# Down projections of a decoder layer: seven half-size products over 16 of 22 weight blocks, with the weight sums made by adding DMAs

## The chip, the cores and the metric

The kernel runs on one core of a Trainium2 chip. The core has a matrix engine (TensorE, "PE" in the profile; "PEld" is its weight load), a vector engine (VectorE, "DVE"), a scalar engine (ScalarE, "ACT"), a general engine (GpSimd, "POOL") and a sequencer that issues DMAs (SyncE, "SP"). Matmuls read SBUF and write PSUM, which has eight banks of 128 x 512 float32. The metric is the device time of one execution in microseconds; smaller is better.

## What is computed

The reference is one layer of a decoder trunk on a sequence of 512 tokens with model width 1024 (float32): a half-step SwiGLU network, a mixer (dilated attention beside an mLSTM, gated and projected), and a second half-step SwiGLU network. The part that matters here is SwiGLU, which stands twice:

```python
def swiglu(x, w_gate, w_up, w_down):
    return (jax.nn.silu(x @ w_gate) * (x @ w_up)) @ w_down

f = swiglu(rmsnorm(x, ffn1_pre_g[l]), ffn1_w_gate[l], ffn1_w_up[l], ffn1_w_down[l])
x = x + 0.5 * rmsnorm(f, ffn1_post_g[l])
```

The inner width is 2816, which is 22 blocks of 128. The down projection is a product of (512 tokens x 2816) with (2816 x 1024).

## The kernel before

**Precision.** Each float32 operand is split in a high part (ScalarE casts it to the matmul's 32-bit type) and a residue (VectorE subtracts the high part). A product is then three matmuls: high x high, residue x high, high x residue. Buffers of high parts are called `wh`, `xh`, `ah`, residues `wl`, `xl`, `al`; each kind has five buffers in turn, and the float32 weight blocks as they land (`wf`, printed `B_a`, `wf_ad`) have three.

**The down stage.** Its output, 512 x 1024, fills all eight banks: four tiles of 128 tokens by two halves of the columns. The names are by quarter of the output: `acca` (tokens 0 to 255, left columns), `accc` (the same tokens, right columns), `accb` (tokens 256 to 511, left), `accd` (those, right). The 22 blocks of the inner width are worked in three ways:

- Blocks 0 to 11 by seven half-size products instead of eight (Strassen's method in Winograd's form). Tokens, inner width and columns are halved. The inner halves are cut in three groups of two blocks each (`HALF = 6`), so there are 7 x 3 products. The string `STEPS` names them: "52" is product 5 of group 2. Product 1 multiplies first-half activations with block (0,0), product 2 second-half activations with block (1,0), product 3 with block (1,1); products 5, 6, 7 and 4 take sums of activation quarters and sums of weight blocks. `sums` makes these sums on VectorE: the weight sums in a tile T (in the place of `hTh`, the transposed input of gate and up, which is used up by then), the activation sums in a tile S.
- Blocks 12 to 14 (`FILL`) as half steps "p" (tokens 0 to 255) and "q" (tokens 256 to 511), strewn among the products.
- Blocks 15 to 21 as plain chunks in `down`: 15 to 17 at once, and the last four (`KEEP`) held back, so that each token tile is finished as a whole and its norm can start.

Every step, a product or a half fill, is twelve matmuls of 128 x 512; a plain chunk is 24.

**What sets the order.** `Down.run` writes the order out by hand: for each step in `STEPS` the load of a later step's block, the sums and casts of the step two ahead, the residues of the next one, the product, and `middle`, which copies or adds finished products among the banks. `Order` (printed as L250, its call) keeps that order on each engine, and each engine works strictly in its order. The first steps are put into the end of the gate/up stage (`seven`, L325, drives them by `next(ahead)`). Loads go on SP's queue. After the stage `down` (L230 is its matmul) does the plain chunks and `PostNorm` (L162, L167), whose gain rows are loaded on GpSimd's queue by `begin`.

Of the kernel before, what the change touches and what calls it, by code (L numbers as in the profile page):

```python
# [39 lines left out]
def tile_hybrid_block(ctx: ExitStack, tc: tile.TileContext, a: dict):  # L40
# [111 lines left out]
    class PostNorm:  # L152
        def __init__(self, t, g, where, name, half=False):
            self.t, self.g, self.name, self.half = t, g, f"p{name}{t}", half
# [3 lines left out]
        def bank(self, acc, b):  # L158
# [3 lines left out]
            nc.vector.tensor_tensor(self.fg[:, BANKS[b]], acc[b], self.g[:, BANKS[b]], op=ALU.mult)  # L162
# [37 lines left out]
    def down(n, chunk_src, get_x, post, finish, todo, name, accs=None, first=0, late=lambda: None):  # L200
        pins = []
        held = []
        accs = accs or [pair(f"acc_{name}{t}") for t in range(NT)]
        for kk in range(first, n):
            xh, xl = get_x(kk)
            wh, wl = load_w(chunk_src(kk), f"{name}d{kk}")
            if kk < n - KEEP:
                for t in range(NT):
                    for b in range(2):
                        step(accs[t][b], xh, xl, wh, wl, t, b, kk == 0, False)  # L210
                    if kk == first and t == 1:
                        late()
# [71 lines left out]
    def seven(do, fs, wgu, x, low, scr, aT, name, ahead):  # L284
# [76 lines left out]
        for i in range(len(fs)):  # L361
# [37 lines left out]
            if w:  # L399
# [11 lines left out]
    LOADS = {"1": ((0, 0),), "2": ((1, 0),), "5": ((0, 1),), "6": ((1, 1),), "7": ((0, 0),), "3": ((1, 1),),  # L411
             "4": ((1, 0),)}
# [4 lines left out]
    class Down:  # L417
        after = FILL[-1] + 1

        def __init__(self, do, wdq, wd, aT, scr, name):  # L420
            self.do, self.wdq, self.wd, self.aT, self.scr, self.name = do, wdq, wd, aT, scr, name
            self.xp, self.src, self.x, self.w, self.wf = None, {}, {}, {}, {}
            self.accs = [[None, None] for _ in range(NT)]
            self.n = 0

        def tt(self, out, p, q, op):
            self.do("vector", "tensor_tensor", out, p, q, op=op)

# [8 lines left out]
        def room(self, n):  # L437
            self.n += 1
            if self.xp and self.n % 2:
                return self.xp.tile([P, 2, T], F32, tag="bf", bufs=3, name=n)  # L440
            return act.tile([P, 2, T], F32, tag="wf", bufs=3, name=n)

        def fetch(self, s):
            if s[0] in "pq":
                t = self.room(f"B{s}_{self.name}").rearrange("p a b -> p (a b)")
                self.do("sync", "dma_start", t, self.wd[FILL[int(s[1])]])
                self.src[s] = self.aT[:, FILL[int(s[1])], None, slice(0, H) if s[0] == "p" else slice(H, T)], halves(t, T)
            for k, j in LOADS.get(s[0], ()):
                t = self.room(f"B{k}{j}_{self.name}{s}")
                self.do("sync", "dma_start", t, halves(self.wdq[int(s[1]), k, j], T))  # L450
                self.wf[s[1], k, j] = t

        def sums(self, s, early=False):
            k, g = s[0], int(s[1])
            if k in "pq":
                return
            A, B = (lambda i, j: self.A(i, j, g)), (lambda i, j: self.wf[s[1], i, j])
            x = A(*{"1": (0, 0), "2": (0, 1), "4": (1, 1)}.get(k, (0, 0)))
            w = B(*{"1": (0, 0), "2": (1, 0), "3": (1, 1)}[k]) if k in "123" else None
            if k in "64":  # L460
                w = self.T[:, 2 * g:2 * g + 2, :]
            if early:
                w = self.scr.tile([P, 2, Q], F32, tag="cd", bufs=1, name=f"t1_{self.name}")
                x = self.scr.tile([P, 2, Q], F32, tag="ab", bufs=1, name=f"s1_{self.name}")[:, :, :H]
            elif k in "57":
                x, w = halves(self.S[:, 7, :], H), self.T[:, 6:8, :]
            if k == "5":
                self.t1, self.s1 = w, x
                self.tt(w, B(0, 1), B(0, 0), SUB)
                self.tt(x, A(1, 0), A(1, 1), ADD)  # L470
            elif k == "6":
                x = halves(self.S[:, g, :], H)
                self.tt(w, B(1, 1), self.t1, SUB)
                self.tt(x, self.s1, A(0, 0), SUB)
            elif k == "7":
                self.tt(w, self.T[:, 2 * g:2 * g + 2, :], B(0, 0), SUB)
                self.tt(x, A(0, 0), A(1, 0), SUB)
            elif k == "3":
                x = work.tile([P, 2, H], F32, tag="s4", bufs=1, name=f"s4_{self.name}{g}")
                self.tt(x, A(0, 1), halves(self.S[:, g, :], H), SUB)  # L480
            elif k == "4":
                self.tt(w, B(1, 0), w, SUB)
            self.src[s] = x, w

        def cast(self, s, which):
# [4 lines left out]
            self.do("scalar", "copy", halves(hl[0], v.shape[2]), v)  # L490
            (self.w if which == "w" else self.x)[s] = hl

        def low(self, s, which):
            v = self.src[s][which == "w"]
            h, l = (halves(y, v.shape[2]) for y in (self.w if which == "w" else self.x)[s])
            self.tt(l, v, h.bitcast(F32), SUB)
# [20 lines left out]
        def middle(self, s):  # L517
            q1, p5 = self.S[:, 3:5, :], self.S[:, 5:7, :]
            for i in range(2):
                if s == "12":  # L520
# [67 lines left out]
    def ffn(pool, todo, first_w, hT, wgu, wdq, wd, post, finish, name, begin=None, pins=(), aT=None):  # L588
# [43 lines left out]
        if begin:  # L632
            begin()
# [883 lines left out]
```

## Time and profile before

| | |
|---|---|
| median of 3 runs | 1346.76 us (1346.64 to 1346.85) |
| the profiled execution | 1346.88 us, its span 1345.1 us, granted TensorE clock 0.999 |
| TensorE busy | 1334.8 us (99%) |
| VectorE busy | 1009.6 us (75%) |
| ScalarE busy | 630.5 us (47%) |
| GpSimd busy | 37.2 us (3%) |

A row of the profile names a line of the kernel, an engine, an operation and tiles as output<-inputs. Tile names end in `_a` in the first FFN and `_b` in the second. A start is in us from the start of the span; "[0.38 <-ACT xh_a L250]" behind a row is idle time of its engine before it and what ended it. Matmuls are pipelined, so that the duration of one (0.39 us for 512 columns) is longer than the distance to the next.

### The profile page before, as it was taken

Reading aid. Unit: us, or ns where it says so; the run is one execution under the profiler, and the core shown is the slowest. Engines: PE = TensorE matmul, PEld = TensorE weight load, DVE = VectorE, ACT = ScalarE, POOL = GpSimd, SP = SyncE. Lnnn points to the kernel's source line nnn. Section 1 sums busy time; section 2 is a strip of 40 time slices with the busy share of each in tenths; the row PEclk is TensorE's granted clock in tenths of the full one; section 3 lists DMA queues with packets and bytes.
Section 4 is the critical chain, followed back from the end, with each engine's and each line's share of the span. In section 5 each row is a group of like instructions: output and inputs, shape, how many; then the busy total and the mean of one; then the engine's idle time right before and its main releaser. Section 6 shows DMA issues by size and latency. Waiting matters only on the chain.

```text
span 1345.1 us, 20741 instructions
## 1 busy us (share of the span) xinstructions
PE 1334.8 (99%) x8319; PEld 1202.5 (89%) x8319; DVE 1009.6 (75%) x1531; ACT 630.5 (47%) x1018; POOL 37.2 (3%) x64
## 2 busy tenths in 40 slices
PE   9999999999999999999999999999999999999998
PEld 8999999878998888888888889999889999998786
DVE  7999897996755557475756676776379998997983
ACT  6444444554643544544544444344265444444552
POOL 1000000000300000000000000000010000000000
PEclk9999999999999999999999999999999999999999
DMA  5333333654433422412222212335312333235441
GB/s 197 99 98 110 110 96 110 234 182 147 128 104 115 142 78 94 156 64 79 79 78 78 79 47 79 103 101 196 134 57 87 109 110 110 95 110 202 173 141 63
DMA packets 42720, 153.96 MB, mean 114 GB/s; under 512 B 4836, under 2 KB 4844, under 8 KB 42368
## 3 DMA queue, kind: packets, MB, share of 16 engines
q1 hardware_dynamic: 39456, 140.56, 31.7%
q0 software_dynamic: 3152, 12.08, 2.7%
q8 instruction: 65, 1.06, 0.3%
q14 instruction: 31, 0.25, 0.1%
q10 hardware_dynamic: 16, 0.00, 0.0%
HBM read 146.33 MB, written 6.29 MB: 113 GB/s over the span
## 4 chain that ended last, share of the span: by engine, by line
PE 90%; DVE 6%; issue 2%; ACT 1%; DMA 0%; DVEq 0%; POOLq 0%; ACTq 0%; SPq 0%
PE qb_b L325 10%; PE qb_a L325 10%; PE pq L175 8%; PE pm L175 7%; PE p L175 6%; PE qa_b L325 4%; PE qa_a L325 4%; PE qb_gm L1075 4%; PE acc_o L230 3%; PE pvo L1201 2%; PE pvo L1203 2%; PE pvo L1202 2%; PE pg_a L189 2%; PE pq L189 2%; PE pg_b L189 2%
## 5 line engine op out<-in xcount | busy, mean ns | idle before, releaser
L175 PE MATMUL pq<-hTh_mx,wh_qk 128*128 128x512 f32 x160 | 63.2, 395 | 0.0
L175 PE MATMUL pq<-hTl_mx,wh_qk 128*128 128x512 f32 x160 | 62.4, 390 | 0.0
L92 DVE TENSOR_TENSOR wl_qk<-wf_qk,wh_qk 128x1024 fp32r<-128x1024 f32 x24 | 29.4, 1223 | 33.3 <-ACT wh_qk L90 16.7
L175 PE MATMUL pm<-hTh_mx,wh_mqk 128*128 128x512 f32 x128 | 50.3, 393 | 0.0
L1201 PE MATMUL pvo<-wh_vo,hTh_mx 128*128 128x512 f32 x128 | 50.2, 392 | 0.0
L175 PE MATMUL pm<-hTl_mx,wh_mqk 128*128 128x512 f32 x128 | 49.9, 390 | 0.0
L1203 PE MATMUL pvo<-wl_vo,hTh_mx 128*128 128x512 f32 x128 | 49.9, 390 | 0.0
L1202 PE MATMUL pvo<-wh_vo,hTl_mx 128*128 128x512 f32 x128 | 49.8, 389 | 0.0
L92 DVE TENSOR_TENSOR wl_mqk<-wf_mqk,wh_mqk 128x1024 fp32r<-128x1024 f32 x16 | 19.6, 1224 | 35.4 <-ACT wh_mqk L90 26.4
L90 ACT CAST wh_qk<-wf_qk 128x1024 fp32r<-128x1024 f32 x24 | 25.0, 1047 | 43.0 <-issue 11.6
L175 PE MATMUL pq<-hTh_mx,wl_qk 128*128 128x512 f32 x160 | 39.6, 389 | 0.0
L250 ACT CAST wh_a<-cd_a 128x1024 fp32r<-128x1024 f32 x19 | 20.0, 1050 | 40.9 <-DVE cd_a L250 40.9
L250 ACT CAST wh_b<-cd_b 128x1024 fp32r<-128x1024 f32 x19 | 20.0, 1050 | 40.5 <-DVE cd_b L250 40.5
L325 PE MATMUL qa_a<-hTh_f,wh_a 128*128 128x256 f32 x152 | 38.2, 284 | 0.0
L325 PE MATMUL qa_b<-hTh_f,wh_b 128*128 128x256 f32 x152 | 38.2, 284 | 0.0
L325 PE MATMUL qa_b<-hTl_f,wh_b 128*128 128x256 f32 x152 | 38.1, 283 | 0.0
L325 PE MATMUL qa_a<-hTl_f,wh_a 128*128 128x256 f32 x152 | 38.1, 283 | 0.0
L996 DVE SCALAR_TENSOR_TENSOR z<-pm,cw,z 128x511 f32<-128x511 f32 (+2 forms) x48 | 35.3, 744 | 1.4 <-ACT z L994 0.9
L90 ACT CAST wh_mqk<-wf_mqk 128x1024 fp32r<-128x1024 f32 x16 | 16.8, 1051 | 41.2 <-PE pvo L1202 22.6
L175 PEld LDWEIGHTS pq<-hTh_mx,wl_qk 128*128 128x128 f32 x160 | 30.0, 188 | 6.2
L175 PEld LDWEIGHTS pq<-hTh_mx,wh_qk 128*128 128x128 f32 x160 | 30.1, 188 | 6.0
L175 PEld LDWEIGHTS pq<-hTl_mx,wh_qk 128*128 128x128 f32 x160 | 30.1, 188 | 6.0
(746 smaller groups left out, 4555.8 us busy)
## 6 DMA issues: line engine op xcount, KB each, us to landing
wf_qk<-in_wqk SPq DMA_DIRECT2D x24, 512.0 KB, 3.3
B_a<-in_wdq SPq DMA_DIRECT2D x21, 512.0 KB, 3.4
B_b<-in_wdq SPq DMA_DIRECT2D x21, 512.0 KB, 3.4
g_a<-in_wgu SPq DMA_DIRECT2D x19, 512.0 KB, 3.8
u_a<-in_wgu SPq DMA_DIRECT2D x19, 512.0 KB, 3.8
g_b<-in_wgu SPq DMA_DIRECT2D x19, 512.0 KB, 3.8
u_b<-in_wgu SPq DMA_DIRECT2D x19, 512.0 KB, 3.7
wf_mqk<-in_wmqk SPq DMA_DIRECT2D x16, 512.0 KB, 3.4
```

The lines of the kernel that those rows point to most:

```text
L90: nc.scalar.copy(wh, wf)
L92: nc.vector.tensor_tensor(wl, wf, wh.bitcast(F32), op=ALU.subtract)
L175: nc.tensor.matmul(out, lhsT=wt[:, k * P:(k + 1) * P], rhs=x[:, k, 0:T], start=n == 0, stop=n == len(terms) - 1)
L189: nc.tensor.matmul(outs[b][:, tok], lhsT=ws_[b][w][:, k * P:(k + 1) * P], rhs=x[:, k, tok], start=i + k + hf == 0, stop=hf == 1 and i == 2 ...
L230: nc.tensor.matmul(out, lhsT=x[:, tk], rhs=w[:, cs], start=first and n == 0, stop=last and n == 2, skip_group_check=True)
L250: self.last[eng] = getattr(getattr(nc, eng), fn)(*args, **kw).ins
L325: nc.tensor.matmul(out, lhsT=wt[:, i * P:(i + 1) * P], rhs=y[:, i, :], start=first and n == 0, stop=last and n == len(terms) - 1, skip_gro ...
L996: nc.vector.scalar_tensor_tensor(z[:, s:], src[:, :T - s], cw[:, ct, 3 - s:4 - s], z[:, s:], op0=ALU.mult, op1=ALU.add)
L1075: nc.tensor.matmul(out, lhsT=wt[:, i * P:(i + 1) * P], rhs=y[:, i, :], start=first and m == 0, stop=last and m == len(terms) - 1, skip_gro ...
L1201: nc.tensor.matmul(out, lhsT=hTh[:, k, tk], rhs=wh[:, cs], start=k == 0, stop=False)
L1202: nc.tensor.matmul(out, lhsT=hTl[:, k, tk], rhs=wh[:, cs], start=False, stop=False)
L1203: nc.tensor.matmul(out, lhsT=hTh[:, k, tk], rhs=wl[:, cs], start=False, stop=k == KD - 1)
```

## The change

Sixteen blocks instead of twelve go through the seven products (`HALF = 8`, four groups: 28 products), two blocks (16 and 17) are half steps, and the last four are plain chunks, all of them held. The signs of the activation sums are turned, and the right half of the output columns is computed with the opposite sign, so that every weight sum is a sum without a minus: 00 + 01 for product 5, that + 11 for product 6, that + 10 for product 4, and 11 + 01 for product 7 ((k,j) is inner half k, column half j). The chain is then made by DMAs that add: block (0,0) is loaded straight into T for product 1; when its residue is made, GpSimd issues a DMA that adds block (0,1) to it in place, and so on. Product 7's chain stands on product 3's block, loaded into four tiles `u3` in the places of scratch tiles. VectorE makes no weight sum any more. Its order is by `front` (sums and casts, three steps ahead) and `back` (residues, two ahead). The fill and plain blocks get their right halves negated in the cast (`flip`), and `PostNorm` multiplies the right bank by -1. `middle` has new places, and `late` is gone. The gains are loaded behind the `u3` loads. `Order`'s line is L263 now, and `step`'s L243.

```diff
-    def load_w(src, name, n=1024, after=()):
+    def cast_w(wh, wf, flip=False):
+        if not flip:
+            return nc.scalar.copy(wh, wf)
+        nc.scalar.copy(wh[:, :T], wf[:, :T])
+        return nc.scalar.mul(wh[:, T:], wf[:, T:], -1.0)
+
+    def load_w(src, name, n=1024, after=(), flip=False):
...
-            nc.scalar.copy(wh, wf)
+            cast_w(wh, wf, flip)
...
-            nc.vector.tensor_tensor(wl, wf, wh.bitcast(F32), op=ALU.subtract)
+            m = T if flip else n
+            nc.vector.tensor_tensor(wl[:, :m], wf[:, :m], wh[:, :m].bitcast(F32), op=ALU.subtract)
+            if flip:
+                nc.vector.scalar_tensor_tensor(wl[:, T:], wf[:, T:], -1.0, wh[:, T:].bitcast(F32), op0=ALU.mult,
+                                               op1=ALU.subtract)
...
-    HALF = 6
-    FILL = (12, 13, 14)
-    STEPS = "20 21 10 50 60 11 51 61 12 52 62 22 p0 p1 70 30 p2 71 31 72 32 40 41 42 q0 q1 q2".split()
...
+    HALF = 8
+    FILL = (16, 17)
+    STEPS = ("20 21 10 11 12 13 22 50 51 52 53 23 60 61 62 63 p0 30 31 32 33 70 71 72 73 p1 "
+             "40 41 42 43 q0 q1").split()
+    BLOCK = {"1": (0, 0), "2": (1, 0), "3": (1, 1), "5": (0, 1), "6": (1, 1), "7": (0, 1), "4": (1, 0)}
...
+        def add(self, s):
+            g = int(s[1])
+            out = halves(self.u3[g], T) if s[0] == "7" else self.U(g)
+            self.do("gpsimd", "dma_start", out, self.B(g, BLOCK[s[0]]), accum_op=ADD)
+
+        def behind(self, s):
+            g = s[1]
+            if s[0] in "153":
+                self.add({"1": "5", "5": "6", "3": "7"}[s[0]] + g)
+            if s == "13":
+                self.fetch("23", "gpsimd")
+            if s == "53":
+                self.fetch("p0", "gpsimd")
+                for g in range(4):
+                    t = self.u3[g] = work.tile([P, D], F32, tag=TEMPS[g], bufs=1, name=f"u3_{self.name}{g}")
+                    self.do("gpsimd", "dma_start", halves(t, T), self.B(g, BLOCK["3"]))
+                if self.begin:
+                    with tc.issue_after(self.do.last["gpsimd"]):
+                        self.begin()
+                self.fetch("p1")
+            if s == "33":
+                for g in range(4):
+                    self.add(f"4{g}")
+                self.fetch("q0")
+                self.fetch("q1")
...
             if k == "5":
-                self.t1, self.s1 = w, x
-                self.tt(w, B(0, 1), B(0, 0), SUB)
-                self.tt(x, A(1, 0), A(1, 1), ADD)
+                self.tt(x, A(1, 1), A(1, 0), SUB)
             elif k == "6":
-                x = halves(self.S[:, g, :], H)
-                self.tt(w, B(1, 1), self.t1, SUB)
-                self.tt(x, self.s1, A(0, 0), SUB)
+                self.stt(x, x, A(0, 0), SUB)
+            elif k == "3":
+                self.stt(x, A(0, 1), x, SUB)
             elif k == "7":
-                self.tt(w, self.T[:, 2 * g:2 * g + 2, :], B(0, 0), SUB)
+                x = work.tile([P, 2, H], F32, tag="s3", bufs=2, name=f"s3_{self.name}{g}")
                 self.tt(x, A(0, 0), A(1, 0), SUB)
...
         def middle(self, s):
...
+            q1, p5 = self.S[:, 4:6, :], self.S[:, 6:8, :]
+            k = {"13": "1", "53": "5", "63": "5", "73": "1", "42": "2", "q1": "6"}.get(s)
+            for i in range(2 if k else 0):
+                out = self.out[k][i]
+                if s in ("13", "53"):
+                    self.do("scalar", "copy", (q1 if s == "13" else p5)[:, i, :], out)
+                elif s in ("63", "73"):
+                    self.tt(out, self.out["6"][i], p5[:, i, :], ADD)
+                else:
+                    self.tt(out, out, q1[:, i, :], ADD)
+            if s == "53":
+                self.tt(p5, p5, q1, ADD)
...
+            for g in range(4):
+                self.do("sync", "dma_start", self.U(g), self.B(g, BLOCK["1"]))
             yield
+            self.added = self.lowered = 2
+            self.front(2)
+            self.back(2)
             self.product(s1)
             yield
+            for n in range(2, len(STEPS)):
+                lead = 2 if n < 5 else 3
+                self.front(n + lead)
+                self.back(n + lead - 1)
                 self.product(STEPS[n])
                 self.middle(STEPS[n])
...
-            return PostNorm(t, gains[0], tbuf[t % 2], "f1", True)
+            return PostNorm(t, gains[0], tbuf[t % 2], "f1", True, True)
```

The instructions move in three places. GpSimd's queue in the first down stage, before: after the opening's last square root (`r_f`) only the two gain rows are loaded, and the next is a constant of the mixer.

```order
L104 TENSOR_TENSOR r_f_223<-s_3_213,nhalf 128x1
L97 DMA g_f1post<-in_ffn_post_g 128x1024
L97 DMA g_mpre<-in_mix_pre_g 128x1024
L1151 DMA selr<-in_sel 4x512
L104 TENSOR_TENSOR r_pf_3755<-v_pf_3753,nhalf 128x1
```

The same place now; the rows onto T are adding DMAs (for products 5, 6 and 4), and so are the second four onto `u` (product 7; the first four are plain loads for product 3).

```order
L263 DMA T_a<-in_wdq 128x1024 x4
L263 DMA B_a<-in_wdq 128x1024
L263 DMA T_a<-in_wdq 128x1024 x4
L263 DMA Bp_a<-in_wd 128x1024
L263 DMA u_a_3158<-in_wdq 128x1024
...
L263 DMA u_a_3164<-in_wdq 128x1024
L107 DMA g_f1post<-in_ffn_post_g 128x1024
L107 DMA g_mpre<-in_mix_pre_g 128x1024
L263 DMA u_a_3158<-in_wdq 128x1024
...
L263 DMA u_a_3164<-in_wdq 128x1024
L263 DMA T_a<-in_wdq 128x1024 x4
```

Twenty-four DMAs stand where two stood, sixteen of them adding ones, and the gains come after the second four adds. VectorE's order before, where group 2's weight sums are made (`T_a<-B_a`) and products 5 and 6 of it prepared (S are activation sums, `wl` and `xl` residues):

```order
L250 TENSOR_TENSOR T_a<-B_a_3063,B_a_3041 128x1024
L250 TENSOR_TENSOR S_a<-aT_a 128x512
L250 TENSOR_TENSOR wl_a<-B_a_3041,wh_a 128x1024
L250 TENSOR_TENSOR xl_a<-aT_a,xh_a 128x512
L250 TENSOR_TENSOR T_a<-B_a_3087,T_a 128x1024
L250 TENSOR_TENSOR S_a<-S_a,aT_a 128x512
L250 TENSOR_TENSOR wl_a<-T_a,wh_a 128x1024
L250 TENSOR_TENSOR xl_a<-S_a,xh_a 128x512
L250 TENSOR_TENSOR wl_a<-T_a,wh_a 128x1024
L250 TENSOR_TENSOR xl_a<-S_a,xh_a 128x512
```

VectorE's order now, from the sum of the two saved products (behind the copy of product 5, step 53) to the banks that step p0 adds into:

```order
L263 TENSOR_TENSOR S_a<-S_a 128x1024
L263 SCALAR_TENSOR_TENSOR S_a<-S_a,aT_a 128x512
L263 TENSOR_TENSOR wl_a<-T_a,wh_a 128x1024
L263 TENSOR_TENSOR xl_a<-S_a,xh_a 128x512
L263 SCALAR_TENSOR_TENSOR S_a<-S_a,aT_a 128x512
...
L263 TENSOR_TENSOR wlp_a<-Bp_a,whp_a 128x512
L263 SCALAR_TENSOR_TENSOR wlp_a<-Bp_a,whp_a 128x512
L263 TENSOR_TENSOR xlp_a<-aT_a,xhp_a 128x256
L263 SCALAR_TENSOR_TENSOR S_a<-aT_a,S_a 128x512
L263 TENSOR_TENSOR wl_a<-u_a_3158,wh_a 128x1024
L263 TENSOR_TENSOR xl_a<-S_a,xh_a 128x512
L263 TENSOR_TENSOR accc_a_2935<-accb_a_2937,S_a 128x512
```

No row makes a weight sum any more; the whole queue behind the saved sum now starts when step 53 is done, and the bank sum of step 63 stands behind the residues of 30.

More of the change, by code (lines that the diff above doesn't have):

```diff
@@ L198, in new_hT, with down @@
         return hTh, hTl
[L200 removed]
+    def down(n, chunk_src, get_x, post, finish, todo, name, accs=None, first=0):
         pins = []
         held = []
+        flip = accs is not None
         accs = accs or [pair(f"acc_{name}{t}") for t in range(NT)]
@@ L489, in cast @@
             hl = [pool.tile([P, n], F32R, tag=f"{tag}{y}", bufs=5, name=f"{which}{y}{s}_{self.name}")[:, :n_] for y in "hl"]
-            self.do("scalar", "copy", halves(hl[0], v.shape[2]), v)
+            h = halves(hl[0], v.shape[2])
+            if which == "w" and s[0] in "pq":
+                self.do("scalar", "copy", h[:, 0, :], v[:, 0, :])
+                self.do("scalar", "mul", h[:, 1, :], v[:, 1, :], -1.0)
+            else:
+                self.do("scalar", "copy", h, v)
             (self.w if which == "w" else self.x)[s] = hl
```

151 lines of the change are left out of this document (57 added, 94 removed).

## The prediction

> **What bounds the kernel now.** I read the page's engine table and chain of waits first, then TensorE's instructions in order of time through the two down stages, then who waited for whom there.
>
> ```profile
> span 1345.1 us, 20741 instructions
> PE 1334.8 (99%) x8319; PEld 1202.5 (89%) x8319; DVE 1009.6 (75%) x1531; ACT 630.5 (47%) x1018; POOL 37.2 (3%) x64
> PE 90%; DVE 6%; issue 2%; ACT 1%; DMA 0%; DVEq 0%; POOLq 0%; ACTq 0%; SPq 0%
> ```
>
> TensorE sets the end: it carries 90% of the chain. So two things alone can change the time: how many matmuls there are, and where TensorE waits. Both stand in the timeline of the down stages (start, duration, matmuls merged in a row):
>
> ```profile
> 236.97 1.09 PE L514 MATMUL acca_a<-wh_a,xh_a 128*128 128x512 f32 x4
> ...
> 241.15 1.09 PE L514 MATMUL acca_a<-wh_a,xh_a 128*128 128x512 f32 x4
> ...
> 243.90 1.07 PE L514 MATMUL accd_a<-wh_a,xh_a 128*128 128x512 f32 x4
> ...
> 246.62 1.07 PE L514 MATMUL accc_a<-wh_a,xh_a 128*128 128x512 f32 x4
> ...
> 256.38 0.50 PE L514 MATMUL accb_a<-wh_a,xh_a 128*128 128x512 f32 x1 [0.38 <-ACT xh_a L250]
> ...
> 314.59 0.39 PE L230 MATMUL acca_a<-wh_ad,ah_a 128*128 128x512 f32 x1
> ...
> 1222.58 0.40 PE L325 MATMUL qb_b<-hTh_f,wl_b 128*128 128x256 f32 x2
> 1222.82 1.09 PE L514 MATMUL acca_b<-wh_b,xh_b 128*128 128x512 f32 x4
> ...
> 1300.43 0.39 PE L230 MATMUL acca_b<-wh_bd,ah_b 128*128 128x512 f32 x1
> ```
>
> Matmuls overlap, so the cost of one is the distance between starts. Step 10 starts at 243.90, the next at 246.62: twelve matmuls take 2.72 us, 0.227 each. From the first down product (236.97) to the first plain chunk (314.59) lie 77.62 us. Work in them: 27 steps x 2.72 = 73.44, and the last gate/up product between the first two steps, 241.15 - 236.97 - 2.72 = 1.46; together 74.90. So TensorE loses 2.72 us here, in small pieces such as the one at 256.38. The second FFN: 1300.43 - 1222.82 = 77.61, lost 2.71.
>
> What those pieces wait for:
>
> ```profile
> 237.00:314.60 77.60, 76.54 (x339) 61.70 (x338) 74.79 (x93) 46.10 (x64) 1.26 (x2) 1.00 0.58 202
> ACT wh_a L250 <- DVE T_a L250: 23.5, 10, 4.0
> PEld accb_a L514 <- ACT xh_a L250: 1.7, 3, 0.8
> ```
>
> The first row is the stage (length; busy PE, PEld, DVE, ACT, POOL; clock, DMA share, GB/s). VectorE is busy 74.79 of 77.60 us, 96%. ScalarE waited 23.5 us in ten waits for weight sums (T) that VectorE makes; TensorE then waits for ScalarE. VectorE is the second bound, and each time its queue runs late TensorE gets a gap.
>
> **The change part by part.**
>
> *Matmuls.* Before: 27 steps of 12 and seven plain chunks of 24, 492. After: 28 products, four half fills (p0, p1, q0, q1), so 32 steps of 12, and four plain chunks: 480. Twelve fewer for each FFN, 12 x 0.227 = 2.72 us, **5.44 us** in both. All lie on TensorE's path.
>
> *VectorE.* Distances between starts again:
>
> ```profile
> 253.45 1.22 DVE L250 TENSOR_TENSOR T_a<-B_a,T_a 128x1024 f32<-128x1024 f32 x1
> 254.58 0.69 DVE L250 TENSOR_TENSOR S_a<-S_a,aT_a 128x512 f32<-128x512 f32 x1
> 255.18 1.22 DVE L250 TENSOR_TENSOR wl_a<-T_a,wh_a 128x1024 fp32r<-128x1024 f32 x1
> ...
> 269.73 1.30 DVE L250 TENSOR_TENSOR accb_a<-accb_a,S_a 128x512 f32<-128x512 f32 x2 [0.56 <-PE accb_a L514]
> 270.93 1.29 DVE L250 TENSOR_TENSOR accc_a<-accb_a,S_a 128x512 f32<-128x512 f32 x2
> ...
> 273.26 0.42 DVE L250 TENSOR_TENSOR xlp_a<-aT_a,xhp_a 128x256 fp32r<-128x256 f32 x1
> 273.59 1.22 DVE L250 TENSOR_TENSOR T_a<-T_a,B_a 128x1024 f32<-128x1024 f32 x1
> ```
>
> 1024 columns take 1.13 us, 512 take 0.60, two bank sums 1.20, a fill's 256 columns 0.33. Gone are twelve weight sums, 12 x 1.13 = 13.6 us for each FFN. After, the stage has 28 weight residues (31.6), 28 activation residues (16.8), four fills of 2 x 0.60 + 0.33 (6.1), 16 activation sums (9.6), one sum of the two saved products (1.1) and eight bank sums (4.8): 70 us in 32 x 2.72 + 1.46 = 88.5 us, 79% where it was 96%. ScalarE stays near its 46.10 of 77.60: the same cast and copy for each step, and a fill's cast in two halves. So the cause of the 2.72 + 2.71 us of gaps is taken away: **5.43 us** at most.
>
> ScalarE's cast and its copy of a finished product's two banks:
>
> ```profile
> 251.30 1.06 ACT L250 CAST wh_a<-T_a 128x1024 fp32r<-128x1024 f32 x1 [1.12 <-DVE T_a L250]
> ...
> 264.94 1.07 ACT L250 COPY S_a<-accd_a 128x512 f32<-128x512 f32 x2
> ```
>
> *The adding DMAs.* They stand off VectorE, but their landing is a new wait, and no row of before shows an adding DMA. The nearest rows (issues on GpSimd's queue, and SP's weight loads; last number: us from issue to landing):
>
> ```profile
> B_a<-in_wdq SPq DMA_DIRECT2D x21, 512.0 KB, 3.4
> xkeep<-x POOLq DMA_DIRECT2D x4, 512.0 KB, 2.9
> v12rows<-v12flat POOLq DMA_DIRECT2D x2, 1024.0 KB, 5.9
> x<-xkeep POOLq DMA_DIRECT2D x4, 512.0 KB, 6.3
> g_mpre<-in_mix_pre_g POOLq DMA_DIRECT2D x1, 512.0 KB, 5.7
> 244.73 0.55 POOL L97 DMA_DIRECT2D g_mpre<-in_mix_pre_g  x1 [2.40 <-DVE aT_a L250]
> ```
>
> An add reads 512 KB of weights and the 512 KB on which they are added. Below, it cannot land sooner than xkeep, 2.9 us, a plain copy alone. Above, the 1024 KB copy, 5.9, plus what company costs (6.3 - 2.9 = 3.4): 9.3. I take **6 to 7 us**, by the 1024 KB copy, which moves as much. The issue costs GpSimd 0.55 us, on an engine with nothing else there.
>
> What may it take? Write 50 for product 5 of group 0. The add for 50 waits until VectorE has made 10's residue, which TensorE wants four matmuls into step 10: 243.90 + 0.91 = 244.8. VectorE then has to do 10's activation residue, three more residue pairs (1.73 each), two activation sums and 22's pair: 0.6 + 5.2 + 1.2 + 1.7 = 8.7, so it comes to 50's residue at 253.5; ScalarE's cast ahead of it takes 1.06. An add that lands by 252.4, after 7.6 us, is not noticed. Slower by s, it delays 50's residue by s, and with it the add for 60, which again takes as long. This second generation meets a wait that is there anyway: VectorE must stop until step 53 is over (243.90 + 9 x 2.72 = 268.4) and its two banks copied (1.07), about 269.6. 60's residue pair has to be done by then: 254.6 + (L - 7.6) + L + 1.06 + 1.73 under 269.6 gives L under about 9.9. Beyond it TensorE pays some 2 us for each us of L in each FFN. So 6 to 7 us costs nothing, nor does 9.3; the whole gain (5.2 per FFN) is gone at about 12.5.
>
> The bandwidth: the stage row has 58% of 77.6 us at 202 GB/s, 15.7 MB or thirty 512 KB transfers at 45/30 = 1.5 us of all sixteen engines. After, 19 plain transfers lie beside the adds in 88.5 us: 28.5 us, so 16 adds fit if one costs under 3.75 us. Two plain transfers would be 3.0: 76.5 of 88.5 us.
>
> No run here shows what the adding itself costs. The Trainium skill ("Collectives: The Full Stack", the bandwidth ceiling in Part 3) says that a reducing DMA runs at about half a copy's rate because it needs two source reads, the addition itself being free. By it, an estimate, an add is two plain transfers, 3.0 us, and nothing is lost.
>
> *First loads.* Group 1's blocks go straight to T, which TensorE frees with its last hTh read (1222.58, done before 1223.0). With 3.4 us of landing, the cast and the residue the first is ready at 1223.0 + 3.4 + 1.06 + 1.22 = 1228.7; step 10 wants it 4.18 + 2.72 + 0.91 after 1222.82, at 1230.6. Hidden by the last gate/up product and step 21. If the load were later than 1.9 us, each us would cost one.
>
> *Two tight places.* (1) Step p0's second half adds into the banks that VectorE updates after step 63. From 269.6 VectorE has the saved sum, three more activation sums up to there and 31's, three residue pairs, p0's and 30's: about 12 us, to 281.7; step 63 ends at 282.0 and p0's second half starts at 283.4, and the first bank sum takes 0.7: it fits by about half a us. (2) All four plain chunks are now held for the end, and the last is wanted 9 matmuls, 2.04 us, after step q1; VectorE has two bank sums (1.20) and one activation residue (0.69) to do after q1 before that: it fits by 0.2 to 0.3. Together I charge **0.25 us for each FFN**, between 0 and 0.5.
>
> *Moved or turned.* The gains' loads go behind the u3 loads on GpSimd, some 20 us later, and are wanted only at the first PostNorm after the held chunks. The turned signs cost VectorE 0.07 us a chunk. In the very last PostNorm the product with -1 is longer, 0.74 against 0.68 by the row of that form:
>
> ```profile
> L996 DVE SCALAR_TENSOR_TENSOR z<-pm,cw,z 128x511 f32<-128x511 f32 (+2 forms) x48 | 35.3, 744 | 1.4 <-ACT z L994 0.9
> ...
> 1339.56 0.68 DVE L162 TENSOR_TENSOR fg_f<-accd_b,g_f2post 128x512 f32<-128x512 f32 x1
> 1340.37 1.41 DVE L167 SCALAR_TENSOR_TENSOR x<-fg_f,r_pf,x 128x512 f32<-128x512 f32 x2
> ```
>
> It ends at 1340.30 where the next starts at 1340.37: hidden.
>
> *Sum.* The profiled execution took 1346.88 us around its span of 1345.1, 0.12 over the median of 1346.76. 1346.88 - 5.44 - 5.43 + 0.50 = 1336.5; against the median **1336.4 us**, 10.4 less, 0.8%.
>
> **The rivals.**
>
> *A, the gaps stay.* TensorE gets its twelve matmuls, but the gaps only change places: the in-order queues now stop for step 53's copy, for p0's banks and for the held chunks, and VectorE's slack there is under half a us. For it: the tight places above. Against: 13.6 us less VectorE work. Full price: 1346.8 - 5.4 = **1341.3**; with half the gaps 1338.6.
>
> *B, the adds are slow: slower than before.* If an add holds the sixteen engines for three plain transfers, 4.5 us, the stage needs 28.5 + 72 = 100.5 us. To the first held chunk the old order needs 77.62 + 3 x 24 x 0.227 = 93.9, the new one ideally 88.5. So it would take 6.6 us more for each FFN: **1360**. It decides from 93.9 = 28.5 + 16c, c = 4.1 us; between 3.75 and 4.1 the gain melts. For it: no row shows an adding DMA, and 16 of them in a stage whose DMA share rises to over 80% queue on each other. Against: the 1024 KB copy of 5.9 us.
>
> *C, the adds land late*, L = 11 to 13 with enough bandwidth: 1.1 to 3.1 us over the limit, 2 us each, twice: 1336.4 + 4.4 to 12.4, about **1345**, no change. Against: 9.3 as the upper bound.
>
> That the change does not do what it says is excluded for the matmuls: the new program has 24 fewer rows on TensorE.
>
> **How the numbers follow.** Forecast 0.68, A 0.15, C 0.05, B 0.12. 0.2% (2.7 us) is about what a measurement here can tell from no change. The forecast and A are faster: 0.83; C is mostly no change: 0.05; B is slower: 0.12. The forecast's own range is 1335.4 (no new gap, and half a us of measurement) to 1338.5; with A and the fast end of C it reaches to 1343, which leaves out B and the rest of C, under 0.2.
>
> **What would show it.** Right: TensorE's stage from the first product to the first held chunk near 88.5 us, VectorE some 80% busy in it, ScalarE's wait for VectorE's T gone; adding DMAs landing in 6 to 7 us, under 9.9. Wrong: ScalarE's casts of T ended by DMA for more than a few us in sum and with them gaps at 50, 60 or 70 (B, C); gaps at p0 and at the first held group (A). The forecast falls if an add takes over 10 us, or if the stage still shows over 1 us of gaps.

## The result, and the profile after

The change takes 1338.58 us (median of 4 runs, 1338.19 to 1338.72) against 1346.80 us of the kernel before (1346.64 to 1347.19): 8.2 us less, a ratio of 0.9938 with a 95% interval of 0.9921 to 0.9955. The forecast was 1336.4 us, in a range of 1335.4 to 1338.5, or to 1343 with rival A and the fast end of C. The sign holds and so does the wider range (the narrow one is missed by 0.1 us), and 2.2 us of the gain are missing. The profile tells where most of them went.

The page of the change, engine table and chain:

```profile
span 1336.6 us, 20773 instructions
PE 1327.0 (99%) x8295; PEld 1199.8 (90%) x8295; DVE 998.6 (75%) x1541; ACT 640.0 (48%) x1042; POOL 71.5 (5%) x108
PE 99%; DVE 0%; DVEq 0%; POOLq 0%; ACT 0%; issue 0%; ACTq 0%
```

TensorE carries 99% of the chain where it was 90%; VectorE's 6% are gone. TensorE's timeline where each of the two stages begins (first product) and ends (first held chunk), and its last matmul:

```profile
237.21 1.09 PE L554 MATMUL acca_a<-wh_a,xh_a 128*128 128x512 f32 x4
...
325.74 0.39 PE L243 MATMUL acca_a<-wh_ad,ah_a 128*128 128x512 f32 x1
...
1217.92 0.86 PE L554 MATMUL acca_b<-wh_b,xh_b 128*128 128x512 f32 x3
...
1306.45 0.39 PE L243 MATMUL acca_b<-wh_bd,ah_b 128*128 128x512 f32 x1
...
1327.98 0.39 PE L243 MATMUL accd_b<-wl_bd,ah_b 128*128 128x512 f32 x1
```

Both stages take 88.53 us. The work in them is 32 x 2.72 + 1.46 = 88.50: of the gaps of 2.72 and 2.71 us only 0.03 is left in each. The last matmul of before, in the same view:

```profile
1338.28 0.39 PE L230 MATMUL accd_b<-wl_bd,ah_b 128*128 128x512 f32 x1
```

TensorE is done 10.30 us earlier. But the span is only 8.5 us shorter, 1345.1 - 1336.6. So 1.8 us were lost after TensorE. The closing instructions of the program show them (duration min/median/max in ns, then first and last start). Before:

```profile
L1513 POOLq EVENT_SEMAPHORE  x4: 17/17/17, 1344.4 to 1345.0; - x4
L1513 POOLq DRAIN  x3: 51/93/2789, 1339.8 to 1344.8; - x3
L1513 SPq DRAIN  x3: 7/7/7, 1344.3 to 1344.6; - x3
```

and in the change:

```profile
L1542 POOLq EVENT_SEMAPHORE  x4: 17/17/17, 1335.9 to 1336.5; - x4
L1542 POOLq DRAIN  x3: 51/98/6381, 1329.5 to 1336.4; - x3
L1542 SPq DRAIN  x3: 7/7/41, 1334.4 to 1336.1; - x3
```

Behind its last instruction (the square root of the last PostNorm) GpSimd's queue stands in an instruction that the profile calls DRAIN. Before, it lasted 2.79 us, to 1342.6, and was over when SP came to its own drain at 1344.3; GpSimd's first closing semaphore followed at once, at 1344.4. In the change GpSimd's drain lasts 6.38 us, to 1335.9. SP comes to its drain at 1334.4 and then waits 1.5 us for GpSimd. The first closing semaphore of GpSimd stands 7.9 us behind the last matmul (1335.9 against 1327.98), where it stood 6.1 us behind it before: these are the 1.8 us. (SP itself came 0.4 us later behind the last matmul than before, 6.4 against 6.0, but GpSimd's drain outlasted that.)

| | us |
|---|---|
| TensorE, first stage with its held chunks, to the mixer's first product (117.52 before, 112.10 now) | -5.42 |
| TensorE, second stage with its held chunks (115.46 before, 110.06 now) | -5.40 |
| opening (+0.24) and mixer (+0.28) | +0.52 |
| end of the program, GpSimd's drain | +1.8 |
| span | -8.5 |

The stages themselves (length; busy PE, PEld, DVE, ACT, POOL; clock, DMA share, GB/s), and the waits of the first that answer to those of before:

```profile
237.20:325.70 88.50, 88.50 (x398) 73.55 (x397) 76.26 (x105) 56.18 (x82) 18.53 (x24) 1.00 0.84 219
1217.90:1306.40 88.50, 88.50 (x398) 73.55 (x397) 76.25 (x105) 56.11 (x82) 17.65 (x23) 1.00 0.79 202
...
ACT wh_a L263 <- DMA T_a<-in_wdq: 11.1, 9, 2.1
ACT wh_a L263 <- DMA u_a<-in_wdq: 3.7, 3, 1.6
```

VectorE is busy 86% of the stage. ScalarE waits for landings of T now (11.1 us in nine waits) and no longer for VectorE's weight sums, and TensorE does not notice: no gap stands behind these waits.

The first FFN's DMA engines over that stage in 40 slices of 2.2 us, busy tenths and GB/s, and the DMA groups (last number: median us to landing):

```profile
DMA  4991899999999999999959599999999500064678
GB/s 120 389 383 56 131 211 193 211 244 333 226 209 209 213 283 333 420 422 413 352 139 183 67 198 206 193 213 209 211 207 241 187 0 0 7 211 141 243 263 289
...
T_a<-in_wdq POOLq DMA_DIRECT2D x12, 512.0 KB, 10.1
u_a<-in_wdq POOLq DMA_DIRECT2D x8, 512.0 KB, 9.0
```

Where the engines are full with plain loads (slices 17 to 19) they move 413 to 422 GB/s, where they are full with adds (slices 28 to 30) 207 to 211. So a 512 KB add holds the sixteen engines for 2.5 us (512 KB at 209 GB/s), twice a plain load's 1.25 (at 418).

### The profile page after: what moved, and what is told of

It is laid out like the page before. It is cut to its first block, busy times and chain, and to the rows that moved or that the text cites. A ratio compares the mean times of both kernels' runs of the same rounds, so it can differ in the third digit from the quotient of the medians.

```text
span 1336.6 us, 20773 instructions
## 1 busy us (share of the span) xinstructions
PE 1327.0 (99%) x8295; PEld 1199.8 (90%) x8295; DVE 998.6 (75%) x1541; ACT 640.0 (48%) x1042; POOL 71.5 (5%) x108
## 4 chain that ended last, share of the span: by engine, by line
PE 99%; DVE 0%; DVEq 0%; POOLq 0%; ACT 0%; issue 0%; ACTq 0%
PE qb_a L338 10%; PE qb_b L338 10%; PE pq L189 8%; PE pm L189 7%; PE p L189 6%; PE qa_a L338 4%; PE qa_b L338 4%; PE qb_gm L1104 4%; PE acc_o L243 3%; PE accb_b L554 2%; PE accb_a L554 2%; PE pvo L1230 2%; PE pvo L1232 2%; PE pvo L1231 2%; PE pq L203 2%; PE pg_a L203 2%
## 5 line engine op out<-in xcount | busy, mean ns | idle before, releaser
L263 ACT CAST wh_a<-cd_a 128x1024 fp32r<-128x1024 f32 x19 | 19.9, 1049 | 40.8 <-DVE cd_a L263 40.8
L263 ACT CAST wh_b<-cd_b 128x1024 fp32r<-128x1024 f32 x19 | 19.9, 1048 | 40.4 <-DVE cd_b L263 40.4
```

What stands on the lines that cost most here:

```text
L263: self.last[eng] = getattr(getattr(nc, eng), fn)(*args, **kw).ins
```

## The experiments

**Was it VectorE's room?** Three kernels. The first is the kernel before with VectorE made lighter: it leaves out the activation residues of products 5, 6, 7 and 4.

```diff
         def low(self, s, which):
+            if which == "x" and s[0] in "5674":
+                self.x[s][1] = self.x[s][0]
+                return
```

> The kernel before with the activation residues of products 5, 6, 7 and 4 left out (TensorE reads the high part in their place, so its work is the same): 12 VectorE instructions of 0.60 us fewer in each FFN, 7.2 us, VectorE at 67.6 of 77.6 us, 87%, as in the change (86%). The weight sums and their hand-over from VectorE to ScalarE stay. Theory 'room': the gaps fall from 2.7 us to under 0.6 for each FFN, time 1346.8 - 4.2 to 5.4 = 1341.4 to 1342.6. Rival 'hand-over': the gaps stay over 2 us, time 1345.4 to 1346.8.

It took 1342.76 us, 4.0 less than before (0.9969, 0.9958 to 0.9981). The stages:

```profile
237.40:312.90 75.50, 75.31 (x338) 61.99 (x337) 68.98 (x81) 46.03 (x64) 1.26 (x2) 1.00 0.59 211
1221.10:1296.70 75.60, 75.41 (x339) 62.04 (x338) 68.84 (x81) 46.02 (x64) 0.57 (x1) 1.00 0.58 203
```

75.56 and 75.58 us from first product to first plain chunk for 74.90 of work: the gaps fell from 2.72 to 0.66 with the weight sums still in place. VectorE is busy 69.0 of 75.5 us there, 91%, not the 87% expected, and gaps and time came out at the edge of theory 'room' (0.66 for 0.6, 1342.76 for 1342.6). It is room that was missing, not the hand-over of sums. Whether the last 0.66 us went in the change by still more room or by its new order isn't shown.

The second fills VectorE in the changed kernel:

```diff
-                self.tt(l, v, h, SUB)
+                for _ in range(2 if which == "x" and s[0] in "5674" else 1):
+                    self.tt(l, v, h, SUB)
```

> The activation residue of products 5, 6, 7 and 4 is made twice with the same values: 16 more VectorE instructions of 0.60 us in each FFN, 9.6 us, which brings VectorE from 76.3 to 85.9 of 88.5 us, 97%, as full as before the change (96%); no weight sum comes back, no DMA changes. Theory 'room' (the gaps of before came from VectorE being full): gaps of 2 to 3 us for each FFN return, time 1338.6 + 4 to 6 = 1343 to 1345. Rival 'hand-over' (the gaps came from the weight sum that stood between landing and cast, not from the load): no gap over 0.3 us, time within 0.6 us of 1338.6.

1340.89 us, 2.3 more than the change and between the two theories; VectorE at 85.6 of 89.8 us, 95%. Gaps came back, but fewer than expected, 1.25 us in each FFN, all at one place, the second half of step p0:

```profile
283.26 0.39 PE L243 MATMUL acca_a<-wlp_a,xhp_a 128*128 128x512 f32 x1
284.57 0.50 PE L243 MATMUL accc_a<-whp_a,xhp_a 128*128 128x512 f32 x1 [0.93 <-DVE accc_a L263]
```

So at nearly the same fullness (96% before) the new order loses under half of what the old one lost; room is the cause, and the order decides where it is missed and how much that costs.

The third puts the weight sums back on VectorE, with plain loads by SP in place of the adds, and keeps the rest of the change:

```diff
-            self.do("gpsimd", "dma_start", out, self.B(g, BLOCK[s[0]]), accum_op=ADD)
+            self.fetch(s)
...
+            if k in "5674":
+                w = halves(self.u3[g], T) if k == "7" else self.U(g)
+                self.tt(w, w, self.wf[s], ADD)
```

> No adding DMA: each of the 16 blocks is loaded by SP into a buffer and VectorE adds it to the same tile (1.13 us each) where the sums of the step are made; matmuls, signs and order stay. VectorE then has 76.3 + 18.1 = 94.4 us of work for 88.5. Theory 'room': the stage is at least 94.4 us, 6 or more us of gaps in each FFN, time 1350 or more, so that the 24 matmuls fewer alone bring no gain over the kernel before (1346.8). Rival 'matmuls alone': VectorE's queue finds room elsewhere, gaps as before the change (2.7 for each FFN), time near 1344.

1347.13 us, the same as before (1.0003, 0.9994 to 1.0012). Stages of 94.06 and 94.04 us, 5.5 us of gaps in each, every one ended by VectorE, the longest here:

```profile
276.58 1.21 PE L557 MATMUL accb_a<-wl_a,xh_a 128*128 128x512 f32 x4 [1.66 <-DVE wl_a L263]
```

So the twenty-four matmuls saved are worth nothing without the adds: they are spent waiting for VectorE. The stage came out as theory 'room' had it; the time is 2.9 us under its 1350, mostly because the 1.8 us at the end of the program are gone too (below).

**What do the adds cost?** Left out:

```diff
-            self.do("gpsimd", "dma_start", out, self.B(g, BLOCK[s[0]]), accum_op=ADD)
```

> The 16 adding DMAs of each FFN are left out, so that the weight sums of products 4 to 7 are just the blocks loaded first; all else stands. Theory (the adds are hidden): TensorE's stage from the first product to the first held chunk stays 88.5 us in both FFNs, and so does every start before the last matmul, within 0.3 us. Rival (the adds cost TensorE something that does not show as a gap): the last matmul starts over 0.5 us sooner than 1327.98. On the end of the program: in the change 1.8 of the 10.3 us won on TensorE were lost after the last output had landed, while GpSimd's final drain took 6.38 us (2.79 before). Theory 'count' (the drain grows with the number of DMAs that GpSimd issued, 26 before, 70 in the change: 0.082 us each): 38 DMAs, drain 3.8 us, no longer the last thing, span 1.4 us shorter, 1335.2, time 1337.1. Rival 'place' (an instruction fetch happens to fall into the end): the drain stays over 6 us or jumps to some other value that does not go with the count.

1336.74 us. The stages stay at 88.52 and 88.53 us: sixteen adds in each cost TensorE nothing inside the stage. The last matmul is 0.64 us sooner, over the rival's 0.5, but that is won in the opening (0.28) and the mixer (0.36), the two stretches of the table above, and several kernels below have the adds without the mixer's loss. The drain:

```profile
L1541 POOLq DRAIN  x3: 51/97/3767, 1329.1 to 1334.6; - x3
```

3.77 us, as the count of DMAs foretold, over at 1332.9 and off the path, since SP comes to its own at 1333.7.

How near the limit the adds are shows when the plain loads between them (block 23, p0, the four u3) go to SP's queue:

```diff
-                self.fetch("23", "gpsimd")
+                self.fetch("23")
...
-                self.fetch("p0", "gpsimd")
+                self.fetch("p0")
...
-                    self.do("gpsimd", "dma_start", halves(t, T), self.B(g, BLOCK["3"]))
+                    self.do("sync", "dma_start", halves(t, T), self.B(g, BLOCK["3"]))
```

> The six plain loads of each FFN that stand on GpSimd's queue (block 23, p0 and the four u3 tiles) go to SP's queue; the adds stay on GpSimd. They land in 3 to 6 us instead of 9 to 14, which TensorE does not notice (stage 88.5 us either way). Theory 'count': 58 DMAs on GpSimd instead of 70, final drain 5.4 us instead of 6.38, span 1.0 us shorter, time near 1337.6. Rival 'place': the drain does not go with the count; time within 0.3 us of 1338.6, or another jump.

1342.14 us, 3.6 slower than the change. The loads start at 239 to 243, 11 to 23 us sooner, and share the DMA engines with the first generation of adds. In the change those of group 0 and group 3 landed after (group 2 took 8.1)

```profile
T_a<-in_wdq POOLq DMA_DIRECT2D x1, 512.0 KB, 5.5
T_a<-in_wdq POOLq DMA_DIRECT2D x1, 512.0 KB, 10.2
```

here those of groups 2 and 3 after

```profile
T_a<-in_wdq POOLq DMA_DIRECT2D x1, 512.0 KB, 15.0
T_a<-in_wdq POOLq DMA_DIRECT2D x1, 512.0 KB, 16.2
```

and step 52, then p0, came late:

```profile
262.02 1.07 PE L554 MATMUL accc_a<-wh_a,xl_a 128*128 128x512 f32 x4
264.12 0.73 PE L554 MATMUL accc_a<-wh_a,xh_a 128*128 128x512 f32 x2 [1.03 <-ACT xh_a L263]
...
285.81 0.50 PE L243 MATMUL accc_a<-whp_a,xhp_a 128*128 128x512 f32 x1 [0.72 <-DVE accc_a L263]
```

The stages took 91.17 and 90.68 us. The drain was 5.40 us (58 DMAs), again as worked out from the count, and its 1 us did not make up for that. I had expected TensorE not to notice the loads' place; it does.

A try at doubling the first generation of adds (those for product 5):

```diff
-            self.do("gpsimd", "dma_start", out, self.B(g, BLOCK[s[0]]), accum_op=ADD)
+            for _ in range(2 if s[0] == "5" else 1):
+                self.do("gpsimd", "dma_start", out, self.B(g, BLOCK[s[0]]), accum_op=ADD)
```

> The adding DMA for product 5 is issued twice in each of the four groups (its weight sum then holds block (0,1) twice), the second waiting for the first; VectorE and TensorE have the same instructions. So the first generation of each chain takes about twice as long, and the DMA engines get four adds more: 28.5 + 20 x 2.6 (measured per add in the change: 128 packets of 4 KB at 328 ns over 16 engines) = 80.5 of 88.5 us. Theory 'limit' (the chain of waits: TensorE notices when first and second generation together take over 19.8 us; the change had about 8 + 10): now 15 to 20 for the first and 10 for the second, 5 to 10 us over, gaps of 5 to 10 us for each FFN at steps 50 to 63, time 1349 to 1359. Rival 'deep cover' (the queues' lead hides more than worked out): gaps under 2 us for each FFN, time under 1343.

1379.75 us in a single run, over 20 us slower than the worst expected. It measured something else than it was meant to: the second add waits on GpSimd's queue for the first to land, and all other adds stand behind it:

```profile
244.21 1.04 POOL L263 DMA_DIRECT2D T_a<-in_wdq  x1 [228.88 <-DVE xl_a L263]
250.09 1.80 POOL L263 DMA_DIRECT2D T_a<-in_wdq  x2 [4.84 <-DMA T_a<-in_wdq]
259.98 1.78 POOL L263 DMA_DIRECT2D T_a<-in_wdq  x2 [8.09 <-DMA T_a<-in_wdq]
```

So it says nothing on the limit of 19.8 us for two generations, but it shows what a wait for a landing does at the head of this queue: one group passes every 6 to 10 us.

**Does the drain go with the number of DMAs?** From the runs so far:

| kernel | DMAs that GpSimd issued | final drain, us |
|---|---|---|
| before | 26 | 2.789 |
| adds left out; sums on VectorE | 38 | 3.767 |
| loads and gains on ScalarE (below) | 55 | 5.157 |
| loads on SP | 58 | 5.401 |
| the change | 70 | 6.381 |

The first and last give 0.0816 us for each; the others fall on that line within 2 ns. That the drain is what the end of the program lost is shown by the kernel with the sums on VectorE: with 38 DMAs its drain is off the path, and from the last matmul to the end of the span it takes 6.80 us, as before the change (6.82), where the change takes 8.62. Without the adds, also 38, it takes 7.56 us: 0.28 more between the last matmul and the last square root, and 0.4 more behind SP's drain, for reasons not found. A test with small ones:

```diff
         nc.gpsimd.dma_start(xkeep[t], xs[t])
+    pad = dram.tile([32, P, 4], F32, name="pad")
+    for i in range(32):
+        nc.gpsimd.dma_start(pad[i], nhalf)
```

> The change with 32 small DMAs more on GpSimd's queue, in the middle of the mixer, hundreds of us before the end (each writes 128 x 4 numbers, 2 KB, to a scratch tensor that nobody reads). Theory 'count' (GpSimd's final drain takes 0.67 us + 0.0816 us for every DMA that GpSimd issued in the whole program; four programs with 26, 38, 58 and 70 gave 2.79, 3.77, 5.40 and 6.38): 102 DMAs, drain 8.99 us, the span 2.6 us longer, time 1341.2. Rival 'volume' (the drain goes with what the DMAs moved, 512 KB each): 32 x 2 KB is nothing, drain 6.4, time 1338.6. Rival 'end' (it goes with what was issued lately): the same 6.4.

1344.91 us and a drain of 5.65 us with 102 DMAs: none of the three. The run with the double adds, 78 DMAs, has 4.22. So the line holds from 26 to 70 DMAs of mostly 512 KB, and beyond that the drain was shorter than the line; why, and whether size matters, stays open. The time is another matter: nothing held the small DMAs in the mixer, and they went to the front of GpSimd's queue, among the opening's square roots; TensorE waited 5.5 us there for VectorE's `h_f`, which waited for one of these.

**The same loads from ScalarE's queue**, to shorten the drain without SP's early start, gains too:

```diff
-                self.fetch("23", "gpsimd")
+                self.fetch("23", "scalar")
...
-                self.fetch("p0", "gpsimd")
+                self.fetch("p0", "scalar")
...
-                    self.do("gpsimd", "dma_start", halves(t, T), self.B(g, BLOCK["3"]))
+                    self.do("scalar", "dma_start", halves(t, T), self.B(g, BLOCK["3"]))
...
+            gains.append(gain(a["mix_pre_g"], "mpre", nc.scalar))
```

> The change with the plain loads of the stage (block 23, p0, the four u3 tiles) and the gain rows issued by ScalarE at the same places of its own order, so that they start when they started on GpSimd's queue, and not at once as on SP's; GpSimd keeps the adds: 55 DMAs. Theory 'count': drain 0.67 + 55 x 0.0816 = 5.16 us, 1.2 us shorter, almost out of the way of SP's end; the stages stay at 88.5 us if the loads take the DMA engines no earlier than before; time 1338.6 - 1.2 = 1337.4. Rival 'traffic' (any load that is not queued behind the adds takes their DMA time): gaps of 1 to 3 us for each FFN at steps 50 to p0 as with SP's queue, time 1339 to 1343.

1340.72 us (one execution of 2721.92 us, unexplained, stands beside four of 1340.4 to 1340.8). Drain 5.16 as expected, second stage 88.61, but 92.44 in the first:

```profile
264.62 0.48 ACTq L107 DMA_DIRECT2D g_f1post<-in_ffn_post_g  x1
269.80 0.34 ACTq L107 DMA_DIRECT2D g_mpre<-in_mix_pre_g  x1
270.25 1.05 ACT L263 CAST wh_a<-T_a 128x1024 fp32r<-128x1024 f32 x1 [5.33 <-DMA Bp_a<-in_wd]
```

ScalarE's queue stood for 5.3 us before the second gain row, until p0's block had landed, and every cast behind it. Neither theory had that. With the gains back on GpSimd (the first three edits of the last diff alone):

> As the run with loads issued by ScalarE, but the gain rows stay on GpSimd's queue (in that run ScalarE stood for 5.3 us in the first FFN before it could issue the second gain row, until p0's block had landed, and 3.9 us of gaps followed; in the second FFN, with one gain row and no such stop, the stage took 88.6 us). GpSimd issues 58 DMAs. Theory 'count': drain 5.40 us, 0.98 us off the end; with the stop gone both stages are 88.5 to 88.7 us; time 1 us under the change, near 1337.6. Rival 'traffic' (the u3 loads take the DMA time of the second generation of adds): gaps of 1 us or more in the first FFN remain, time 1338.6 or more.

1338.02 us; drain 5.40, second stage 88.70, first 89.42, with one gap of 0.9 us at p0:

```profile
283.09 0.39 PE L243 MATMUL acca_a<-wlp_a,xhp_a 128*128 128x512 f32 x1
284.04 0.50 PE L243 MATMUL accc_a<-whp_a,xhp_a 128*128 128x512 f32 x1 [0.56 <-DVE accc_a L263]
...
u_a<-in_wdq ACTq DMA_DIRECT2D x4, 512.0 KB, 15.8
```

Between the two theories: the drain's 1 us is won, and most of it given back to traffic. Beside it ran the change again:

> The change itself, unaltered, on the same chip and beside the same runs of the kernel before. The profile of the change lost 0.2 us against the kernel before in the opening and 0.3 us at the first projections of the mixer, where the program is the same. If this belongs to the program, it is there again, stage starts 237.2 and 1217.9, time 1338.6; if it is chance of an execution, the stages start near 236.97 and 1217.4.

1338.43 us, stages 88.52 and 88.53, the drain 6.38 again. The loss in the mixer came again, of the opening's 0.24 us only 0.06: that part was chance of an execution. From its first product to the second stage the mixer takes 868.6 us in both executions of the change and in the run with residues made twice, 868.2 to 868.3 in the kernel before and in the changed kernels with the adds left out, the sums on VectorE, or the loads on SP or ScalarE. The adds alone don't make it, then. But the run with the small DMAs, which has adds and loads on GpSimd's queue as the change has, doesn't show it either (868.3), and its cause stays open.

Last, the u3 loads on ScalarE only when the second generation of adds is nearly through:

```diff
-                for g in range(4):
-                    t = self.u3[g] = work.tile([P, D], F32, tag=TEMPS[g], bufs=1, name=f"u3_{self.name}{g}")
-                    self.do("gpsimd", "dma_start", halves(t, T), self.B(g, BLOCK["3"]))
...
+            if s == "61":
+                for g in range(4):
+                    t = self.u3[g] = work.tile([P, D], F32, tag=TEMPS[g], bufs=1, name=f"u3_{self.name}{g}")
+                    self.do("scalar", "dma_start", halves(t, T), self.B(g, BLOCK["3"]))
```

> As the run with loads issued by ScalarE and gains on GpSimd, but ScalarE issues the four u3 loads one step-pair later, when the residue of step 61 is due (some 8 us later, about 272 in the first FFN), so that they no longer share the DMA engines with the second generation of adds, which delayed 63's cast by 3.2 us there and left 0.9 us of gap at p0. Theory 'traffic' (that sharing made the gap): no gap over 0.2 us in either stage, 58 DMAs on GpSimd, drain 5.40 us, time 1337.5, 1 us under the change. Rival 'the loads are wanted sooner': they land too late for step 30, gaps of 1 us or more there, time over 1338.6.

1337.03 us (1336.86 to 1337.12), and with "62" in the place of "61":

> The same with the u3 loads issued when the residue of step 62 is due, another 2 to 3 us later. Theory 'traffic': as the run beside it, no gap, time 1337.5. Rival 'the loads are wanted sooner': here first, with a gap at step 30 of up to 2 us for each FFN, time 1338 to 1341.

1336.86 us (1336.76 to 1337.02), ratio 0.9926 (0.9912 to 0.9940): 1.6 us under the change's 1338.43 in the run above, with ranges apart and the kernel before at 1346.77 and 1346.85 beside them. No gap in either stage (88.52 and 88.53):

```profile
237.00:325.50 88.50, 88.50 (x398) 73.49 (x398) 76.52 (x105) 55.64 (x83) 15.35 (x18) 1.00 0.84 219
...
u_a<-in_wdq ACTq DMA_DIRECT2D x4, 512.0 KB, 6.9
...
L1543 POOLq DRAIN  x3: 51/93/5401, 1328.9 to 1334.8; - x3
```

The u3 loads land in 6.9 us where they took 15.8 in the run with the earlier issue, and the drain is 1 us shorter. So traffic was the cause of the gap at p0, and this version beats both kernels: against the change in the run above, 1.0 us behind the last matmul and 0.3 us in the mixer, whose loss it doesn't have.

## Why the prediction was right, and where it was off

- **Matmuls, 5.44 us**, and **VectorE's room, 5.43 us**: both came, 10.82 us on TensorE. The cause named for the gaps, a full VectorE, is shown by the lighter kernel before (gaps 2.72 to 0.66) and by the sums put back (5.5).
- **VectorE's load** was put at 79% and is 86%. The 70 us left out the residues of the held chunks that lie inside the stage, eleven of 0.60 us from start to start:

```profile
L99 DVE TENSOR_TENSOR wl_ad<-wf_ad,wh_ad 128x512 fp32r<-128x512 f32 x4 | 2.7, 686 | 0.8 <-ACT wh_ad L86 0.8
L669 DVE TENSOR_TENSOR al_a<-aT_a,ah_a 128x512 fp32r<-128x512 f32 x4 | 2.7, 683 | 0.0
L101 DVE SCALAR_TENSOR_TENSOR wl_ad<-wf_ad,wh_ad 128x512 fp32r<-128x512 f32 x3 | 2.0, 683 | 0.0
```

- **The adds' landing, 6 to 7 us**, was mis-sized: 5.5 for the first, 10 for most others. One add alone is a little quicker than supposed; the adds of four groups follow each other every 1.7 us and each holds the engines for 2.5, so they queue. The step that failed is the single L (landing time) for all; the limits of 7.6 and 9.9 us were worked out for group 0, whose add meets an empty queue, and the later groups have more lead: it took the 15.0 us of group 2, in the run with loads on SP, to cost 1.2 us at step 52. So "the forecast falls if an add takes over 10 us" was wrong. Casts of T ended by DMA for 11.1 us in sum, named there as a sign of B and C, came without the gaps that were to come with them.
- **The bandwidth** was taken too dear: 3.0 us for an add, measured 2.5, and 1.5 for a plain load, measured 1.25; the share of 84 and 79% is under the forecast's 86. The Trainium skill ("Collectives: The Full Stack", the bandwidth ceiling in Part 3) states for the reduce step of a collective that it runs at about half a copy's rate; the trace of these adding loads agrees: 207 to 211 against 413 to 422 GB/s.
- **The tight places**, 0.25 us for each FFN, cost nothing. But p0 is where it gives way: all six kernels of the new order that have gaps have one of 0.9 to 1.5 us there in the first FFN. At the held chunks none was seen. Rival A's mechanism is real, with some room left. That its time with half the gaps, 1338.6, is the measured one is chance: no gap stayed.
- **The end of the program** is the term that was missing, and 1.8 of the 2.2 us with it: I took what lies behind the last matmul as fixed, apart from 0.06 us for PostNorm's product with -1 (it took 0.68 us, as before). The forty-four DMAs more on GpSimd were costed by their issue alone ("an engine with nothing else there"); they also lengthen its final drain by 3.6 us, of which 1.8 show.
- **The opening and the mixer** lost 0.52 us that no term foresaw, 0.28 of it in the mixer, where the program is the same.
- By these terms: 10.82 - 0.52 - 1.8 = 8.5 us of span. On TensorE the forecast's 10.87 - 0.50 is right to 0.1 us, but by luck: the 0.50 charged for the tight places wasn't spent, and the 0.52 of opening and mixer wasn't foreseen. Behind TensorE it was wrong.

## What to carry to other kernels

Work moved off a full engine pays only where that engine's fullness makes the gaps, so try it by making the engine lighter before building the replacement. Adding DMAs made these sums at no cost to TensorE because the adds had a lead of some 10 us; what else loaded at that time had to be queued behind them or wait until they were through. Count the DMAs on GpSimd's queue against the end of the program, and look at the drain behind its last instruction.

## What was not expected of the hardware

- GpSimd's final drain took 0.67 us plus 0.0816 us for every DMA it had issued in the whole program, from 26 to 70; with 78 and 102 it took 4.22 and 5.65 us, less than the line, unexplained.
- An adding DMA moved half the bytes a second of a plain one (207 to 211 against 413 to 422 GB/s, in the DMA slices of the first stage).
- Plain loads behind adds on GpSimd's queue landed only after 11 to 14 us, and this did no harm: on SP's queue, at once, the same loads made the adds late (15.0 us for group 2, 8.1 in the change), and on ScalarE's queue, at the same places, they left a gap at p0.

```profile
B_a<-in_wdq POOLq DMA_DIRECT2D x1, 512.0 KB, 11.5
g_f1post<-in_ffn_post_g POOLq DMA_DIRECT2D x1, 512.0 KB, 13.7
```

- After the 6.9 us stop in the run with double adds, TensorE was granted about half its clock (0.55, where it was 1.00 ahead of the stop) for the next four us, so that this gap cost more than itself (the two rows of stages are length; busy PE, PEld, DVE, ACT, POOL; clock, DMA share, GB/s):

```profile
255.00:259.00 4.00, 4.00 (x19) 3.29 (x18) 2.29 (x3) 1.57 (x2) 0.00 (x0) 1.00 0.98 253
...
267.19 2.08 PE L555 MATMUL accc_a<-wh_a,xh_a 128*128 128x512 f32 x4 [6.89 <-ACT xh_a L263]
...
267.20:271.30 4.10, 4.10 (x10) 3.28 (x11) 1.87 (x3) 0.90 (x2) 1.78 (x2) 0.55 0.41 47
```
